# A new order of the seven products of a block, and norm statistics issued two chunks later, in a decoder step of two layers

## Chip, cores and metric

One core of a Trainium2 chip runs the whole step. The metric is device time in microseconds (us), the median of several executions. Engines are named as in the profile: PE (TensorE, matrix products), DVE (VectorE), ACT (ScalarE), POOL (GpSimd), SP (the queue that issues DMAs).

## What is computed

The reference is one inference step of a two-layer decoder for 1024 prompt tokens and 8 samples of 4 tokens, 1056 columns in all, in fp32. Each layer has a recurrent mixer, a cross attention and a feed-forward part with a causal convolution of width 3:

```python
def conv_ffn(h, w_up, conv_w, conv_b, w_down, prev):
    L = h.shape[1]
    up = h @ w_up
    ext = jnp.concatenate([prev.astype(up.dtype), up], axis=1)
    c = conv_b + conv_w[0] * ext[:, 0:L]
    for j in range(1, CONV_W):
        c = c + conv_w[j] * ext[:, j:j + L]
    a, b = jnp.split(c, 2, axis=-1)
    y = (jax.nn.silu(a) * b).astype(h.dtype)
    return y @ w_down, ext[:, L:]
```

`h` is the RMS norm of the 1024-wide residual stream, `w_up` is 1024 x 5632, `w_down` 2816 x 1024. The last two columns of `ext` are the convolution states that are returned.

## The kernel before

**Blocks of seven products.** The feed-forward products go through Strassen's scheme in Winograd's form: a 2x2 block product is made of seven products of sums of blocks. A unit is one pair of 128 output rows. In the up projection (tiles `blu`) there are 21 units a layer, f = 1 to 21, of four 128-row slices of each operand half; in the down projection (`bld`) 20 units a layer, of two slices. The operands are split in a high and a low fp32r part, so each 128x128 piece takes three matmuls (`mm3`, lines 592 to 594). A product has two halves c of 264 columns; one half is a step: 4 x 3 = 12 matmuls in an up unit, 6 in a down unit. A unit has 14 steps, in the order of the list `ORDER` (line 46), run by `products` (line 694).

**Banks.** `PRODUCTS` gives each product its accumulation bank q. Products 1, 6, 7 and 4 add up in bank 0, one after the other, and after each one the sum so far is read out; product 2 has bank 1; products 5 and 3 share bank 2. A product that adds to a bank can't start before the sum that stands there has been read. The reading is `take` in `ffn_take` (up) and `ffn_add` (down): in an up unit ACT copies (line 961), DVE adds (965) and POOL multiplies by the norm factor (966), or DVE does both for product 4 (963). In a down unit DVE adds to the residual (981), or for products 1 and 6 ACT copies (978) and POOL adds (979).

**Weights of the next unit.** `Blocks.steps` is called after each step of a unit and prepares the next one: POOL makes the sums s2, s3 (lines 231, 233), s1 (232) and s4 (237); `parts` splits them, ACT casting the high part (217) and DVE subtracting (218). The tiles `whi/wlo` rotate over two buffers, shared by a11, a12 and by s2, s3; s1, a22 have slots of their own (`wh1/wl1`).

**Convolution of the unit before.** `ffn_conv` queues for each half of the columns an ACT pass (`ct`, line 1002), two DVE multiply-adds a side (1005), the SiLU on ACT (1009), a DVE product (1011) and a store of the row to HBM (`fd`). These are handed out in `tick` as credit of PE time builds up.

**The order on each engine** is not that of the code alone: the framework's scheduler replays the program against its own model and places an instruction where that model finds it ready. Every engine then works through its list strictly in order.

**Norm statistics.** The factor of the feed-forward norm isn't known when the first up projections (`pju`, by `proj`, four chunks of 264 columns each) start. `proj` issues the sums of squares (`stats`, tiles `npsff`) after its first chunk, and `spread` (tiles `dgff`, `nbcff`) after the last chunk of the first projection; the chunks' results wait in their banks until then.

**States.** `conv_state_out` and `conv_last` transpose the convolution states on PE (tiles `cops`) and store them; the last two are issued in the first and the second down unit, in `ffn`.

Of the kernel before, what the change touches and what calls it, by code (L numbers as in the profile page):

```python
# [26 lines left out]
T = TP + TS  # L27
NCH = 3
CH = T // NCH
H = T // 2  # L30
HC = H // 2
# [11 lines left out]


PRODUCTS = {1: ("a11", "b11", 0), 2: ("a12", "b21", 1), 3: ("s4", "b22", 2), 4: ("a22", "t4", 0), 5: ("s1", "t1", 2), 6: ("s2", "t2", 0), 7: ("s3", "t3", 0)}
ORDER = [(1, 0), (1, 1), (2, 0), (6, 0), (6, 1), (2, 1), (7, 0), (7, 1), (5, 0), (5, 1), (4, 0), (4, 1), (3, 0), (3, 1)]
STARTS = (1, 2, 5)
GROUPS = [2,2,2,2,2]
OH = 3
# [1 line left out]
OP = 3  # L51
OB = 3
OG = 2
PREP = {(0, 2): 1, (1, 3): 2, (1, 10): 1, (2, 3): 1, (2, 8): 1, (2, 11): 1, (3, 0): 1, (3, 4): 1, (3, 10): 1, (3, 12): 1}
RL = 2
PA, PB = (2, 6)
# [21 lines left out]
class Task:  # L78


    def __init__(self, gen):
        self.gen, self.done, self.result = gen, False, None
        self.step()
# [119 lines left out]
class Blocks:  # L203
# [19 lines left out]
    def steps(self, at):  # L223
        k, w, n = self.k, self.w, self.name
        gt = k.nc.gpsimd.tensor_tensor
        wt = lambda q: k.wp.tile([P, 1024], F32R, tag=q, name=f"{q}{n}", bufs=2)[:, :2 * w]
        for s in at:
            a, b = self.raw
            if s == 2:
                self.s = k.c(f"ws{n}")[:, :2 * w]  # L230
                gt(out=self.s[:, w:], in0=a[:, :w], in1=b[:, :w], op=ALU.subtract)  # L231
                gt(out=b[:, :w], in0=b[:, :w], in1=b[:, w:], op=ALU.add)  # L232
                gt(out=self.s[:, :w], in0=b[:, :w], in1=a[:, :w], op=ALU.subtract)
            elif s == 6:
                self.parts(a, ("a11", "a12"), wt("whi"), wt("wlo"))
            elif s == 7:
                gt(out=a[:, w:], in0=a[:, w:], in1=self.s[:, :w], op=ALU.subtract)
            elif s == 9:
                t = k.wp.tile([P, 1024], F32R, tag="whi", name=f"whs{n}", bufs=2), k.wp.tile([P, 1024], F32R, tag="wlo", name=f"wls{n}", bufs=2)
                self.parts(self.s, ("s2", "s3"), t[0][:, :2 * w], t[1][:, :2 * w])  # L240
            elif s == 11:
                self.parts(b, ("s1", "a22"), k.c(f"wh1{n}", F32R)[:, :2 * w], k.c(f"wl1{n}", F32R)[:, :2 * w])
            elif s == 12:
                t = k.c(f"w4{n}", F32R)
                self.parts(a[:, w:], ("s4",), t[:, :w], t[:, w:2 * w])
# [39 lines left out]
class Kernel:  # L285
    def __init__(self, tc, ins, outs):
        self.tc, self.nc = tc, tc.nc
        self.i, self.o = ins, outs
        self.fill = []
        self.planned, self.ready = [], {}  # L290
        self.slow, self.credit = [], 0.0
        self.chain, self.owed = None, 0.0
        self.pending = None
        self.vcol = {}
        self.wide, self.odd = False, 0

# [98 lines left out]
    def v(self, nm, j):  # L395
        return self.vcol[nm][:, j:j + 1]
# [199 lines left out]
    def proj(self, w, col, hi, lo, evac, name, width=P, ch=CH):  # L596

        n = len(hi)
        us = 3 * n * ch / 2400.0
        wh, wl = self.wunit(self.wcol(w, col, n, name, width))  # L600
        held = []
        for c in range(T // ch):
            sl = slice(c * ch, (c + 1) * ch)
            ps = self.abank(f"pj{name}{c}")
            for k in range(n):
                self.mm3(ps[:width, :ch], wh[:, k], wl[:, k], hi[k][:, sl], lo[k][:, sl], k == 0, k == n - 1)
            if c == 1:
                self.prefetch()
            if self.pending is None:
                evac(c, ps)  # L610
            else:
                held.append((c, ps))
                if c == 0:
                    self.pending.stats(self.pending.tokens())
                elif c == T // ch - 1:
                    self.pending.spread()
                    self.pending = None
                    for q in held:
                        evac(*q)
            self.tick(us - 0.6)  # L620
            yield us

# [71 lines left out]
    def products(self, weights, acts, n, name, take):  # L694
# [3 lines left out]
        us = 3 * n * HC / 2400.0  # L698
        for s, (p, c) in enumerate(ORDER):
            a, b, q = PRODUCTS[p]  # L700
# [84 lines left out]
    def ffn(self, l, norm, ahead, cuts=None, post=None):  # L785
# [12 lines left out]
        at = 0  # L798
# [55 lines left out]
        for u, (g, m, w) in enumerate(dns):  # L854
            t = self.c(f"dt{w.name}") if SLOWADD else None
            g.run()
            i = groups.index(g) + 1
            for s in self.products(w, g.acts, g.n, w.name, self.ffn_add(m, t)):
                self.ahead(todo, len(ups) + u, s)
                if i < len(groups):  # L860
                    groups[i].run(PREP.get((m // 2, s), 0))
                if u == 0 and s == 6:
                    self.conv_state_out(l, NFT - NFT % 4)
                if u == 1 and s == 6:
                    self.conv_last(l)
                if u == len(dns) - 1 and s == 10:
                    self.tick(1e9)
                    last = self.ffn_rest(l, at)
                yield
# [82 lines left out]
    def ffn_take(self, exts, rstd):  # L952
        nc = self.nc

        def take(p, c, ps):
            q, h = {1: (0, 0), 2: (0, 0), 6: (0, 1), 3: (0, 1), 7: (1, 1), 5: (1, 1), 4: (1, 0)}[p]
            a = h * H + c * HC
            for d, s, v in self.pieces(exts[q], a, HC):
                z, r = v(ps[:, s]), v(rstd[:, a + s.start:a + s.stop])
                if p in (1, 6, 7):  # L960
                    nc.scalar.copy(out=d, in_=z)  # L961
                elif p == 4:
                    nc.vector.tensor_tensor(out=d, in0=z, in1=r, op=ALU.mult)
                else:
                    nc.vector.tensor_tensor(out=d, in0=d, in1=z, op=ALU.add)  # L965
                    nc.gpsimd.tensor_tensor(out=d, in0=d, in1=r, op=ALU.mult)  # L966
            return 0.0 if p in (1, 6, 7) else 0.4
        return take

    def ffn_add(self, m, t):  # L970
# [655 lines left out]
    def heads(self, nm, cur, proj, gates, gname, s0, sp, ss, last, before=None):  # L1626

        self.pt = self.tok(f"pt{nm}")
        self.nc.gpsimd.memset(self.pt, 0.0)
        lz = self.c(f"lz{nm}")  # L1630
        self.nc.gpsimd.memset(lz[:, :1024], 0.0)
        self.ph = lz[:, 512:768].rearrange("p (c i) -> p c i", i=32)
        self.lq = lz[:, :NS * 32].rearrange("p (s c) -> p s c", c=32)
        self.lp = lz[:TS, NS * 32:NS * 32 + 2 * P]
        res = []
        for h in range(4):
            q, k, g, vt, vts = cur
            n = f"{nm}{h}"
            if before is not None:
                before(h)  # L1640
            gt = self.later(gates(h))
            nxt = self.later(proj(h + 1)) if h < 3 else last(res)
            res.append(self.lin(q, k, g, vt, vts, gt, gname, s0[0, :, h], sp[0, 0, h], ss[0, :, h], n))
            if h < 3:
                while not nxt.done:
                    self.gap(1.0)
                cur = nxt.result
        return res
# [8 lines left out]
    def mix_six(self, w, os_, y):  # L1657
        self.plan(self.wrow(w, 4 * P, 2, "mo14"))
        yield 0.0
        yield from self.out_six(w, os_, "mo1", y, OG)  # L1660

# [5 lines left out]
    def gla(self):  # L1667
        rstd = self.next
        hi, lo = rstd.hi, rstd.lo
        self.gla_gate_load()  # L1670
        self.spill()
        w = self.i["w_out_c"][0]

        def last(res):
            os_ = [t for o in res for t in o]
            y = [self.split(t, f"mo1{4 + j}") for j, t in enumerate(os_[4:])]
            self.fill[0].finish()
            self.fill.pop(0)
            self.reload("mx1")
            self.later(self.mix_six(w, os_, y))  # L1680
        proj = lambda h: self.gla_proj(h, hi, lo, rstd)
        gates = lambda h: self.gates(self.i["w_in_c"][0], 2048 + h * 256, 2, hi, lo, rstd, f"gl{h}")
        res = self.heads("gl", self.run(proj(0)), proj, gates, "gla_gnorm", self.i["state_gla"], self.o["gla_p"], self.o["gla_s"], last)
        self.mix_last(w, 6, res[3], 1)
# [570 lines left out]
```

## Time and profile before

| | |
|---|---|
| median of 3 runs | 3276.51 us (3275.88 to 3279.37) |
| the profiled execution | 3273.8 us, its span 3272.0 us |
| PE busy | 3104.0 us, 95% |
| DVE busy | 2427.9 us, 74% |
| ACT / POOL busy | 1460.5 / 1458.8 us |
| mean granted PE clock | 0.984 of full |

The profile shows one execution. Busy shares are means over stages of different kinds, so a stage is read through its own stretch of time. Up units of layer 0 run from 961 to 1412 us, its down units from 1412 to 1656; in layer 1 from 2530 to 2973 and to 3230.

### The profile page before, as it was taken

The page shows a single profiled execution, that of the slowest core. Times are in us where ns is not written, and L with a number is a line of the kernel's source. Part 1 is how long each engine was busy: PE and PEld are TensorE (multiplying, and loading weights), DVE is VectorE, ACT ScalarE, POOL GpSimd, SP SyncE. Part 2 cuts the span into 40 slices and gives each one's busy share as a digit, 9 for nine tenths or more (in the row PEclk, how much of TensorE's full clock was granted, in tenths as well). Part 3 has the DMA queues.
Part 4 walks back from the last instruction along what each step waited for, and adds up shares of the span by engine and source line. Part 5 has one row for each costly group of instructions (what it writes and reads, how often), then busy time and mean ns, then how long its engine had stood idle before and what let it go on. Part 6 is the DMA issues. An engine that isn't in the chain of part 4 may idle for free.

```text
span 3272.0 us, 65208 instructions
## 1 busy us (share of the span) xinstructions
PE 3104.0 (95%) x25741; PEld 2953.6 (90%) x25741; DVE 2427.9 (74%) x4662; ACT 1460.5 (45%) x3008; POOL 1458.8 (45%) x1722
## 2 busy tenths in 40 slices
PE   8999899999989999989999999899999999998998
PEld 7998888998889999988899999889988999998888
DVE  6649977844798887799984444684379977878998
ACT  7122265444464444444443334244446544444445
POOL 4011113200467677778731111340035777678774
PEclk9999999999999999999999999999999999999999
DMA  8513264344222222243231111225332222224322
GB/s 263 186 47 96 84 208 152 112 137 151 78 87 84 79 79 76 71 144 99 79 124 49 50 57 57 79 71 187 101 130 86 87 70 80 77 77 148 99 72 96
DMA packets 367072, 336.07 MB, mean 103 GB/s; under 512 B 30030, under 2 KB 317949, under 8 KB 366765
## 3 DMA queue, kind: packets, MB, share of 16 engines
q1 hardware_dynamic: 366764, 331.90, 31.7%
q8 instruction: 202, 3.31, 0.4%
q14 instruction: 106, 0.86, 0.1%
HBM read 250.60 MB, written 81.24 MB: 101 GB/s over the span
## 4 chain that ended last, share of the span: by engine, by line
PE 49%; DVE 28%; POOL 10%; issue 6%; ACT 5%; DMA 1%; DVEq 0%; SPq 0%; ACTq 0%; POOLq 0%
DVE ct L1005 5%; POOL ext L966 3%; DVE xff L981 2%; PE blu L592 2%; PE pjxq L594 2%; PE pjxq L592 2%; PE pjxq L593 2%; PE blu L594 2%; PE blu L593 2%; ACT ct L1002 2%; DVE ext L965 1%; DVE wlsu L218 1%; POOL wsu L231 1%; POOL wru L232 1%; ACT ct L1009 1%
## 5 line engine op out<-in xcount | busy, mean ns | idle before, releaser
L966 POOL TENSOR_TENSOR ext<-ext,rstdff 128x264 f32<-128x264 f32 (+2 forms) x336 | 299.2, 903 | 207.6 <-DVE ext L965 207.6
L1005 DVE SCALAR_TENSOR_TENSOR ct<-ext,cw,ct 128x528 f32<-128x528 f32 (+1 forms) x352 | 329.0, 956 | 47.2 <-ACT ct L1002 46.4
L979 POOL TENSOR_TENSOR xff<-xff,dtd 128x264 f32<-128x264 f32 x160 | 162.7, 1031 | 74.6 <-ACT dtd L978 74.4
L1002 ACT ACTIVATE ct<-ext,cw 128x544 f32<-128x544 f32 (+1 forms) x176 | 141.3, 830 | 115.6 <-POOL ext L966 83.7
L592 PE MATMUL blu<-hhff,whiu 128*128 128x264 f32 x672 | 192.1, 286 | 0.0
L594 PE MATMUL blu<-hhff,wlou 128*128 128x264 f32 x672 | 191.6, 286 | 0.0
L720 POOL TENSOR_TENSOR o<-o 128x528 f32<-128x528 f32 x4 | 5.4, 1342 | 361.1 <-DVE xo0bb L270 180.5
L981 DVE TENSOR_TENSOR xff<-xff,bld 128x264 f32<-128x264 f32 x400 | 155.5, 418 | 11.3 <-PE bld L594 6.8
L592 PEld LDWEIGHTS blu<-hhff,whiu 128*128 128x128 f32 x672 | 127.9, 190 | 0.0
L594 PEld LDWEIGHTS blu<-hhff,wlou 128*128 128x128 f32 x672 | 127.5, 190 | 0.0
L592 PE MATMUL pjxq<-hhxa,whxq 128*128 128x352 f32 x384 | 126.4, 329 | 0.0
L593 PE MATMUL pjxq<-hlxa,whxq 128*128 128x352 f32 x384 | 125.5, 327 | 0.0
L594 PE MATMUL pjxq<-hhxa,wlxq 128*128 128x352 f32 x384 | 124.9, 325 | 0.0
L965 DVE TENSOR_TENSOR ext<-ext,blu 128x264 f32<-128x264 f32 (+2 forms) x336 | 111.0, 351 | 10.3 <-PE blu L594 5.5
L1009 ACT ACTIVATE ct<-ct 128x528 f32<-128x528 f32 x88 | 57.3, 651 | 136.1 <-DVE ct L1005 136.0
L961 ACT COPY ext<-blu 128x264 f32<-128x264 f32 (+2 forms) x336 | 94.7, 322 | 48.3 <-PE blu L594 48.2
L592 PE MATMUL blu<-hhff,w4u 128*128 128x264 f32 x336 | 96.2, 286 | 4.4 <-DVE ext L965 4.4
L1011 DVE TENSOR_TENSOR ct<-ct 128x528 f32<-128x528 f32 x88 | 88.4, 1005 | 13.1 <-ACT ct L1009 13.1
L593 PE MATMUL blu<-hhff,whiu 128*128 128x264 f32 x336 | 97.0, 289 | 0.0
L593 PE MATMUL blu<-hlff,whiu 128*128 128x264 f32 x336 | 95.6, 284 | 0.0
L594 PE MATMUL blu<-hhff,w4u 128*128 128x264 f32 x336 | 95.5, 284 | 0.0
L593 PE MATMUL blu<-hlff,w4u 128*128 128x264 f32 x336 | 95.5, 284 | 0.0
(2690 smaller groups left out, 13067.0 us busy)
## 6 DMA issues: line engine op xcount, KB each, us to landing
wru<-in_ffn_w_up SPq DMA_DIRECT2D x88, 512.0 KB
wrd<-in_ffn_w_down SPq DMA_DIRECT2D x80, 256.0 KB
wrkv<-in_xa_w_kv SPq DMA_DIRECT2D x32, 512.0 KB
kc<-in_cache_mem_k SPq DMA_DIRECT2D x64, 256.0 KB
vc<-in_cache_mem_v SPq DMA_DIRECT2D x64, 256.0 KB
fd<-ct SPq DMA_DIRECT2D x44, 264.0 KB
fd<-ct SPq DMA_DIRECT2D x44, 248.0 KB
xmx<-xd SPq DMA_DIRECT2D x16, 528.0 KB
```

What stands on the lines that cost most here:

```text
L592: nc.tensor.matmul(ps, wh, ah, start=first, stop=False, **kw)
L593: nc.tensor.matmul(ps, wh, al, start=False, stop=False, **kw)
L594: nc.tensor.matmul(ps, wl, ah, start=False, stop=last, **kw)
L961: nc.scalar.copy(out=d, in_=z)
L965: nc.vector.tensor_tensor(out=d, in0=d, in1=z, op=ALU.add)
L966: nc.gpsimd.tensor_tensor(out=d, in0=d, in1=r, op=ALU.mult)
L979: nc.gpsimd.tensor_tensor(out=x, in0=x, in1=b, op=ALU.add)
L981: nc.vector.tensor_tensor(out=x, in0=x, in1=ps, op=ALU.add)
L1002: nc.scalar.activation(out=ct[q], in_=exts[q][0][:, o:o + w], func=AF.Identity, scale=wv(0, q), bias=wv(3, q))
L1005: nc.vector.scalar_tensor_tensor(out=ct[q], in0=exts[q][0][:, o + j:o + j + w], scalar=wv(j, q), in1=ct[q], op0=ALU.mult, op1=ALU.add)
L1009: nc.scalar.activation(out=a, in_=a, func=AF.Silu)
L1011: nc.vector.tensor_tensor(out=b[:, :n], in0=a[:, :n], in1=b[:, :n], op=ALU.mult)
```

## The change

It reorders the seven products to 1, 2, 6, 5, 7, 3, 4, both halves of one after the other. So a bank's next product stands three steps behind the end of the one before. With product 5 ahead of product 7, its sum is the first that lands in its quarter: in `ffn_take` ACT now copies product 5's and DVE adds product 7's. In `Blocks.steps` the splits of s2, s3 and of s1, a22 change places. In `proj` the statistics come after the third chunk and the spreading after the first chunk of the second projection where chunks are 264 wide (`HC`); for 352 wide chunks (`CH`) nothing changes. The last state transposes go from the first and second down unit to the third and fourth.

```diff
-ORDER = [(1, 0), (1, 1), (2, 0), (6, 0), (6, 1), (2, 1), (7, 0), (7, 1), (5, 0), (5, 1), (4, 0), (4, 1), (3, 0), (3, 1)]
+ORDER = [(p, c) for p in (1, 2, 6, 5, 7, 3, 4) for c in (0, 1)]
...
+STATS, SPREAD = {CH: 0, HC: 2}, {CH: 2, HC: 4}
...
-            elif s == 9:
+            elif s == 11:
                 t = k.wp.tile([P, 1024], F32R, tag="whi", name=f"whs{n}", bufs=2), k.wp.tile([P, 1024], F32R, tag="wlo", name=f"wls{n}", bufs=2)
                 self.parts(self.s, ("s2", "s3"), t[0][:, :2 * w], t[1][:, :2 * w])
-            elif s == 11:
+            elif s == 9:
                 self.parts(b, ("s1", "a22"), k.c(f"wh1{n}", F32R)[:, :2 * w], k.c(f"wl1{n}", F32R)[:, :2 * w])
...
-                held.append((c, ps))
-                if c == 0:
+                self.held.append((evac, c, ps))
+                at = len(self.held) - 1
+                if at == STATS[ch]:
                     self.pending.stats(self.pending.tokens())
-                elif c == T // ch - 1:
+                elif at == SPREAD[ch]:
                     self.pending.spread()
                     self.pending = None
-                    for q in held:
-                        evac(*q)
+                    while self.held:
+                        f, *q = self.held.pop(0)
+                        f(*q)
...
-                if u == 0 and s == 6:
+                if u == 2 and s == 6:
                     self.conv_state_out(l, NFT - NFT % 4)
-                if u == 1 and s == 6:
+                if u == 3 and s == 6:
                     self.conv_last(l)
...
-                if p in (1, 6, 7):
+                if p in (1, 6, 5):
                     nc.scalar.copy(out=d, in_=z)
...
-            return 0.0 if p in (1, 6, 7) else 0.4
+            return 0.0 if p in (1, 6, 5) else 0.4
```

ACT in up unit 6 of layer 0, before. `blu_600` and `blu_601` are the halves of bank 0 of unit 6, `ext_12401` and `ext_12404` its two sides, `wh1u_7` and `whiu_7` weights of unit 7, `ct` the convolution of unit 5. The second pair of copies from bank 0 reads product 6, the third product 7:

```order
L961 COPY ext_12401<-blu_600_12407 128x264
L1002 ACTIVATE ct_12460<-ext_12145,cw_10715 128x544
L961 COPY ext_12401<-blu_601_12426 128x264
L217 CAST wh1u_7_12618<-wru_71_12395 128x1024
L1009 ACTIVATE ct_12460<-ct_12460 128x544
L961 COPY ext_12401<-blu_600_12407 128x264
L961 COPY ext_12401<-blu_601_12426 128x232
L961 COPY ext_12401<-blu_601_12426 128x8x4
L217 CAST whiu_7_12533<-wru_70_12211 128x1024
L961 COPY ext_12404<-blu_600_12407 128x264
```

The same place in the change (`blu_620` is product 5):

```order
L964 COPY ext_12401<-blu_600_12407 128x264
L1012 ACTIVATE ct_12460<-ct_12460 128x544
L219 CAST wh1u_7_12588<-wru_71_12395 128x1024
L964 COPY ext_12401<-blu_601_12426 128x264
L219 CAST whiu_7_12534<-wru_70_12211 128x1024
L964 COPY ext_12401<-blu_600_12407 128x264
L964 COPY ext_12401<-blu_601_12426 128x232
L964 COPY ext_12401<-blu_601_12426 128x8x4
L964 COPY ext_12404<-blu_620_12520 128x264
L219 CAST w4u_7_12639<-wru_70_12211 128x512
```

The cast `wh1u`, which stood ahead of the copies of product 6, now stands ahead of the second copy of product 1, and `whiu` ahead of product 6's.

DVE near the end of up unit 6, before (`blu_620`, `blu_621`: bank 2, first product 5, further down product 3):

```order
L965 TENSOR_TENSOR ext_12404<-ext_12404,blu_620_12556 128x264
L218 TENSOR_TENSOR wlsu_7_12589<-wsu_7_12463,whsu_7_12588 128x1024
L218 TENSOR_TENSOR w4u_7_12636<-wru_70_12211,w4u_7_12636 128x512
L965 TENSOR_TENSOR ext_12404<-ext_12404,blu_621_12571 128x232
L965 TENSOR_TENSOR ext_12404<-ext_12404,blu_621_12571 128x8x4
L1005 SCALAR_TENSOR_TENSOR ct_12681<-ext_12401,cw_10715,ct_12681 128x528
L963 TENSOR_TENSOR ext_12404<-blu_600_12407,rstdff_10894 128x264
L1005 SCALAR_TENSOR_TENSOR ct_12681<-ext_12401,cw_10715,ct_12681 128x528
L963 TENSOR_TENSOR ext_12404<-blu_601_12426,rstdff_10894 128x264
L965 TENSOR_TENSOR ext_12401<-ext_12401,blu_620_12556 128x264
```

The same place in the change (`blu_600`, `blu_601` first product 7, further down product 4):

```order
L220 TENSOR_TENSOR w4u_7_12639<-wru_70_12211,w4u_7_12639 128x512
L968 TENSOR_TENSOR ext_12404<-ext_12404,blu_600_12407 128x264
L968 TENSOR_TENSOR ext_12404<-ext_12404,blu_601_12426 128x232
L968 TENSOR_TENSOR ext_12404<-ext_12404,blu_601_12426 128x8x4
L220 TENSOR_TENSOR wlsu_7_12623<-wsu_7_12463,whsu_7_12622 128x1024
L968 TENSOR_TENSOR ext_12401<-ext_12401,blu_620_12520 128x264
L968 TENSOR_TENSOR ext_12401<-ext_12401,blu_621_12542 128x232
L968 TENSOR_TENSOR ext_12401<-ext_12401,blu_621_12542 128x8x4
L1008 SCALAR_TENSOR_TENSOR ct_12681<-ext_12401,cw_10715,ct_12681 128x528 x2
L966 TENSOR_TENSOR ext_12404<-blu_600_12407,rstdff_10921 128x264
```

Product 3's adds have moved ahead of product 4's, so the unit's last reading is one that POOL takes no part in. `wlsu` stands behind the adds of product 7.

PE at the third group of sums of squares in layer 0, before:

```order
L593 MATMUL pju_03_10869<-hlff_10311,whu_0_10612 128x264
L159 MATMUL npsff_10789<-ones,sqaff_10313 128x2 x3
L594 MATMUL pju_03_10869<-hhff_10303,wlu_0_10613 128x264
L592 MATMUL pju_03_10869<-hhff_10304,whu_0_10612 128x264
L593 MATMUL pju_03_10869<-hlff_10312,whu_0_10612 128x264
```

and in the change:

```order
L595 MATMUL pju_03_10869<-hlff_10311,whu_0_10612 128x264
L161 MATMUL npsff_10845<-ones,sqaff_10313 128x2 x3
L596 MATMUL pju_03_10869<-hhff_10303,wlu_0_10613 128x264
L594 MATMUL pju_03_10869<-hhff_10304,whu_0_10612 128x264
L595 MATMUL pju_03_10869<-hlff_10312,whu_0_10612 128x264
```

The group stands between the same two matmuls in both. Only the second group and the spreading (`nbcff`, 11 and 24 matmuls) have moved back.

## Rows read from the trace of the kernel before

**Rows 1.** The page: span, then busy time of each engine.
```profile
span 3272.0 us, 65208 instructions
...
PE 3104.0 (95%) x25741; PEld 2953.6 (90%) x25741; DVE 2427.9 (74%) x4662; ACT 1460.5 (45%) x3008; POOL 1458.8 (45%) x1722
```

**Rows 2.** Who waited for whom on PE: total us, times, longest us.
```profile
PE bld L592 <- DVE xff L981: 30.7, 32, 1.3
PE blu L592 <- ACT ext L961: 30.5, 25, 1.5
PE npsff L159 <- DVE sqaff L133: 11.5, 2, 5.8
...
PE cops L778 <- POOL cst L991: 6.9, 2, 3.5
```

**Rows 3.** Windows: up units 4 to 20, down units and their starts, layers 0, 1.
```profile
core 0: us, PE busy (x) PEld busy (x) DVE busy (x) ACT busy (x) POOL busy (x), PEclk, DMA share, GB/s
1032.20:1395.90 363.70, 351.41 (x2867) 349.30 (x2866) 291.28 (x437) 169.29 (x309) 260.20 (x341) 1.00 0.24 76
1410.00:1656.00 246.00, 221.09 (x1712) 213.31 (x1712) 229.54 (x383) 108.11 (x235) 187.18 (x185) 0.99 0.32 107
1425.00:1460.00 35.00, 30.62 (x230) 29.58 (x230) 30.78 (x49) 13.78 (x32) 31.20 (x30) 0.95 0.29 98
2597.90:2962.00 364.10, 351.47 (x2867) 349.33 (x2866) 291.06 (x438) 168.08 (x307) 261.17 (x341) 1.00 0.25 76
2973.00:3222.00 249.00, 224.53 (x1730) 217.35 (x1729) 231.96 (x384) 110.15 (x240) 189.56 (x187) 0.98 0.32 106
2990.00:3040.00 50.00, 41.77 (x321) 40.48 (x319) 45.50 (x75) 23.92 (x52) 40.29 (x40) 0.97 0.28 91
```

**Rows 4.** Windows cut at the first matmul of up units 7, 8, 9, 10.
```profile
1097.30:1117.80 20.50, 20.50 (x170) 20.50 (x170) 15.60 (x24) 8.10 (x17) 13.35 (x19) 1.00 0.26 79
1117.80:1140.00 22.20, 20.75 (x171) 20.53 (x170) 18.28 (x29) 11.55 (x21) 17.06 (x21) 1.00 0.25 79
1140.00:1160.40 20.40, 20.40 (x170) 20.40 (x169) 16.05 (x24) 8.20 (x17) 13.22 (x19) 1.00 0.25 80
1160.40:1182.60 22.20, 20.84 (x172) 20.62 (x171) 18.29 (x29) 11.57 (x21) 17.04 (x21) 1.00 0.23 73
sum 85.30, PE 82.48 PEld 82.06 DVE 68.22 ACT 39.42 POOL 60.66; mean PE 20.62 PEld 20.51 DVE 17.06 ACT 9.85 POOL 15.17
```

**Rows 5.** Timeline of unit 8, PE: start us, us, [idle before <-releaser].
```profile
1128.83 0.39 PE L592 MATMUL blu<-ff0t00h,whsu 128*128 128x264 f32 x1 [1.45 <-ACT ext L961]
```

**Rows 6.** The same timeline, ACT.
```profile
1122.12 0.85 ACT L1002 ACTIVATE ct<-ext,cw 128x544 f32<-128x544 f32 x1 [2.07 <-POOL ext L966]
...
1126.91 1.05 ACT L217 CAST wh1u<-wru 128x1024 fp32r<-128x1024 f32 x1 [3.68 <-POOL wru L232]
1127.86 0.65 ACT L1009 ACTIVATE ct<-ct 128x544 f32<-128x544 f32 x1
1128.42 0.71 ACT L961 COPY ext<-blu 128x264 f32<-128x264 f32 x3
```

**Rows 7.** The same timeline, POOL.
```profile
1123.31 1.83 POOL L231 TENSOR_TENSOR wsu<-wru,wru 128x512 f32<-128x512 f32 x1
1125.21 1.66 POOL L232 TENSOR_TENSOR wru<-wru 128x512 f32<-128x512 f32 x1
```

**Rows 8.** Waits of DVE, up units of layer 0: total us, times, longest us.
```profile
DVE ct L1005 <- ACT ct L1002: 21.4, 34, 1.6
...
DVE w4u L218 <- ACT w4u L217: 16.9, 8, 2.1
```

**Rows 9.** Two lines of DVE: duration ns min/median/max, first and last start.
```profile
L1005 DVE SCALAR_TENSOR_TENSOR ct<-ext,cw,ct x352: 751/777/1811, 976.4 to 3213.2; 128x528 f32<-128x528 f32 x126, 128x544 f32<-128x544 f32 x50
...
L965 DVE TENSOR_TENSOR ext<-ext,blu x336: 171/402/433, 975.8 to 2991.4; 128x264 f32<-128x264 f32 x84, 128x32 f32<-128x32 f32 x42, 128x232 f32<-128x232 f32 x42
```

**Rows 10.** Timeline of the start of layer 0's up projection, PE.
```profile
942.16 1.44 PE L159 MATMUL npsff<-ones,sqaff 128*128 128x2 f32 x6 [5.74 <-DVE sqaff L133]
...
952.91 0.49 PE L183 MATMUL nbcff<-dgff,ones 128*128 128x128 f32 x2 [1.17 <-DVE dgff L176]
...
970.54 0.39 PE L594 MATMUL blu<-ff0t00h,wl1u 128*128 128x264 f32 x1 [1.86 <-DVE wl1u L218]
```

More of the change, by code (lines that the diff above doesn't have):

```diff
@@ L292, in __init__ @@
         self.chain, self.owed = None, 0.0
-        self.pending = None
+        self.pending, self.held = None, []
         self.vcol = {}
@@ L600, in proj @@
         wh, wl = self.wunit(self.wcol(w, col, n, name, width))
-        held = []
         for c in range(T // ch):
```

## The prediction

> **What bounds the kernel now.** First the page's engine line: PE is busy 3104.0 us of 3272.0, DVE 2427.9 [rows 1]. So the most that better ordering can give is the 168 us in which PE idles, and only what this change touches of them. Second, the list of PE's waits [rows 2]: the entries that the change can touch are `bld` on DVE (30.7 us), `blu` on ACT's copies (30.5), `npsff` on DVE (11.5) and `cops` on POOL (6.9). The mixers' Strassen products run in the same order, and none of their tiles is in these rows: I put them at nothing.
>
> Third, the stretches. In up units 4 to 20 PE is busy 351.4 of 363.7 us, 21.39 a unit, with the clock at 1.00 [rows 3]. Cut at each unit's first matmul, the units alternate: 20.50, 22.20, 20.40, 22.20 us [rows 4]. The short ones are PE's floor, 168 matmuls without a gap, 0.122 us each, 1.46 us a step. The long ones idle at one place: 1.45 us ahead of product 7, for ACT's copy of product 6 [rows 5]. Why is that copy late? ACT's list says it: the copies stand behind the cast `wh1u`, which waited 3.68 us for POOL's sum `wru` [rows 6], and that sum ended at 1125.21 + 1.66 = 1126.87, 9.07 us after the unit's start at 1117.80, behind `wsu` of 1.83 us [rows 7]. So the up stage is not short of any engine; one engine's list is in an unlucky order in every second unit.
>
> The down stage is another case: DVE is busy 229.5 of 246.0 us and 232.0 of 249.0, PE only 221.1 and 224.5 [rows 3]. DVE is the bound there, and only its own idle time, 16.5 + 17.0 = 33.5 us, can be had.
>
> **The change, up units.** The old order alternates because the scheduler placed conv work of the unit before differently in even and odd units; the new one has all units alike. Product 7 now comes behind product 5: 36 matmuls (4.4 us) lie between product 6's end and product 7's start, where there were 29 (3.5 us) in the long units, counted in PE's list. The sum `wru` itself comes earlier: POOL reaches it after the unit before has its readings behind it, and product 3's adds come two steps, 2.9 us, sooner. From 9.07 that makes 6.15 us after the unit's start. Now the new list on ACT: `wh1u` stands ahead of the second copy of product 1, which releases the second half of product 6, 61 matmuls or 7.45 us into the unit. The cast takes 1.05 us [rows 6], one half's copy 0.36, half of the 0.71 for three pieces of which the first is one half [rows 6]; so `wru` may end until about 6.0 us. 6.15 against 6.0: this is close, a stall of 0.15 us a unit at worst in this reckoning, and none if odd units' earlier start holds.
>
> With PE free, who is next? DVE. Its busy time in a unit is 15.60 to 18.29, mean 17.06 us [rows 4]. To that come waits its list holds by itself: for ACT's `ct` pass 21.4 us over 17 units, 1.26 a unit, and for ACT's part of `w4u` 16.9 over 8, 2.1 each [rows 8]. 17.06 + 1.26 + 2.1 = 20.4. If the two halves' `ct` passes of 0.85 us each [rows 6] are both waited for in full, 1.7 takes the place of 1.26: 20.9. I take 20.7 between the two, just above PE's floor. So a unit goes from 21.39 to 20.7, −0.69; over 36 units (the 34 of both windows and one more a layer from those at the ends) −25 us. Bounds: PE's floor of 20.5 gives −0.89 x 36 = −32; no gain gives 0; the losses are among the rivals.
>
> The swap of the two `parts` calls moves the ACT casts and DVE subtractions `wlsu`, 1024 wide, behind product 7's adds; it issues the same instructions. The copies of product 5 on ACT and the adds of product 7 on DVE are the old ones of 7 and 5 with names exchanged: nothing. No DMA is added; POOL's and SP's lists keep their entries.
>
> **Down units.** The same order there; a unit's readings by DVE don't get fewer. What goes is what idles DVE. The last `cops` transposes make PE wait 3.5 us twice [rows 2]; around them DVE idles 35.0 − 30.78 = 4.2 and 50.0 − 45.5 = 4.5 us [rows 3], because it has no product to read. Two units later, POOL's `cst` will be long done: −8.7. Of the other 25 us of DVE's idle time I count 1.3, since product 3 no longer follows on the bank of product 5 with only two steps between: −10 together. Bounds: 0, and −20 if half of the rest goes as well. That the clock is granted at 0.95 and 0.97 around the transposes [rows 3] would add about a microsecond; it stays inside these bounds.
>
> **Head of the feed-forward.** The third group of sums of squares stands between the same two matmuls as before, so its wait of 5.74 us for `sqaff` [rows 10] stays, twice. The second group and the spreading move 11 and 24 matmuls back; the spreading's wait of 1.17 us would go, but the first `blu` matmul waits 1.86 us for `wl1u` at 970.54 behind it [rows 10], and what is saved ahead is waited there. So 0, with −11.5 (both waits gone) as the other end.
>
> **Sum.** 3273.8 (the profiled execution) − 25 − 10 = 3238.8. The median of the runs, 3276.5, lies 2.7 above that execution: 3241.
>
> **Rivals.**
>
> *DVE's round becomes the bound, and the kernel is slower.* The long units carry 18.28 us of DVE work, the short ones 15.60 [rows 4], since multiply-adds (L1005) move from one to the other and their price changes: 751 ns at the least, 777 in the middle, 1811 at the most, while the adds of L965, which have one input from a bank, never pass 433 [rows 9]. If the even order puts every unit at 18.28, the round is 18.28 + 1.7 + 2.1 = 22.1, +0.7 a unit: +25 − 10, 3291 us. It decides from a DVE round of 21.4. For it: product 5's `wlsu` and the multiply-adds now stand together while POOL makes the weight sums. Against it: the mean of two units carries the same instructions, and readings moved ahead leave `ct` nothing new to wait for. The Trainium skill ("SBUF — State Buffer", Who interferes with whom) has the mechanism: a DVE instruction with two SBUF inputs contends with a GpSimd instruction that reads SBUF. The trace agrees in kind (1811 against 433 ns [rows 9]); by that rule alone the round would lie nearer 22.1 than 20.7, as more of those multiply-adds would meet POOL's sums.
>
> *ACT's head is blocked in every unit.* If `wru` still ends 9.07 us into the unit, the cast ends at 10.1, and product 6's second half, wanted at 7.45, starts at 10.5: 3.0 us lost in each, 23.5 a unit, +76 − 10, 3342 us. It decides from `wru` ending at 6.9 us, where the loss equals today's mean stall of 0.89. Against it: product 3's adds come 2.9 us sooner.
>
> *PE's floor.* DVE follows without trouble in the short units (15.60 and 16.05 of 20.4); if so in all, −32, and the down stage gives 15 to 20: about 3224.
>
> *Only the down stage gains.* ACT's wait is replaced by another of the same length, at product 5 or 3: 3273.8 − 10 + 2.7 = 3266.
>
> *The statistics don't do what is said.* The later issue moves the group of 5.74 us past no matmul; this is in the forecast already, at nothing.
>
> **How the numbers follow.** Forecast with its own range (3228 to 3256): 0.55. PE's floor: 0.15. Only the down stage: 0.13. DVE's round: 0.12. ACT's head: 0.05. The range 3212 to 3272 takes the first three and what the bounds of the head can add below (3224 − 11.5); the two slower cases, 0.17, are left out. A measurement of this kernel tells 0.2%, 6.5 us, from no change: below 3270 is faster, above 3283 slower. From the third case 0.03 goes to no change, and 0.02 from the edge of the fourth: faster 0.80, same 0.05, slower 0.15.
>
> **What would show it.** Right: up units all alike at 20.5 to 20.9 us in the windows, `blu` on ACT's `ext` under 5 us in the list of PE's waits, `cops` on `cst` gone, `npsff` still at 11.5, down stages of about 241 and 244 us, DVE busy around 17 us in each up unit. Wrong: alternating units, a new entry of `blu` waiting for DVE's `ext` over 20 us (first rival), `wru` ending later than 6.9 us after a unit's start with PE idle ahead of product 6's second half (second), or a median outside 3212 to 3272.

## The result and the profile after

| | before | after |
|---|---|---|
| median of 4 runs each | 3276.2 us (3272.98 to 3279.37) | 3242.48 us (3238.84 to 3243.13) |
| ratio, 95% interval | | 0.9895 [0.9878, 0.9912] |
| the profiled execution, its span | 3273.8, 3272.0 us | 3238.8, 3237.1 us |

The two profiled executions lie 35.0 us apart, the medians 33.7. First the page of the change, with the lines that answer to [rows 1]:

```profile
span 3237.1 us, 65350 instructions
...
PE 3101.1 (96%) x25741; PEld 2952.3 (91%) x25741; DVE 2446.9 (76%) x4662; ACT 1454.7 (45%) x3008; POOL 1468.3 (45%) x1722
```

PE does the same work; DVE is busy 19 us longer with the same 4662 instructions. Next the list of PE's waits, as in [rows 2] (total us, times, longest us):

```profile
PE bld L596 <- DVE wlod L220: 15.0, 13, 2.0
PE npsff L161 <- DVE sqaff L135: 12.0, 2, 6.3
PE bld L594 <- DVE xff L984: 10.6, 10, 1.7
PE bld L594 <- ACT whid L219: 7.9, 3, 3.9
...
PE blu L596 <- DVE wl1u L220: 6.5, 2, 3.3
```

The waits of `blu` for ACT's `ext` (30.5 us before) are 2.0 us now, below the rows shown. `cops` is gone; a wait of 3.9 us of `bld` for ACT's `whid` is new. `npsff` stays. Where the time went is read from windows that begin at the same instructions in both traces. In the kernel before, up units 1 to 3 and then unit 21 with the down units, layer 0 and layer 1 (columns as in [rows 3]):

```profile
961.16:1032.17 71.01, 65.06 (x508) 63.48 (x506) 68.51 (x90) 36.95 (x65) 53.34 (x63) 0.98 0.26 79
1395.91:1662.20 266.29, 241.28 (x1869) 233.13 (x1868) 247.71 (x412) 119.24 (x257) 198.41 (x196) 0.99 0.34 112
2529.49:2600.48 70.99, 65.95 (x508) 64.52 (x507) 68.47 (x90) 37.03 (x65) 53.35 (x63) 0.95 0.25 78
2964.64:3230.40 265.76, 241.29 (x1863) 234.11 (x1862) 247.14 (x409) 117.99 (x254) 197.47 (x196) 0.98 0.32 107
```

In the change, with the stretch of up units 4 to 20 of layer 0 and layer 1, which answers to [rows 3], as the second and fifth line:

```profile
954.81:1028.16 73.35, 66.28 (x508) 65.01 (x507) 69.24 (x96) 37.97 (x67) 51.86 (x68) 0.95 0.27 80
...
1028.16:1379.56 351.40, 351.07 (x2867) 349.65 (x2866) 299.62 (x436) 166.06 (x306) 268.03 (x343) 1.00 0.26 78
...
1379.56:1639.50 259.94, 240.34 (x1864) 234.38 (x1862) 246.28 (x410) 118.49 (x255) 197.18 (x195) 0.97 0.34 114
2512.78:2586.24 73.46, 65.55 (x507) 64.28 (x506) 69.52 (x96) 38.01 (x68) 51.88 (x68) 0.95 0.26 80
...
2586.24:2937.53 351.29, 350.98 (x2867) 349.74 (x2866) 300.77 (x436) 166.04 (x306) 269.27 (x343) 1.00 0.26 78
...
2937.53:3195.00 257.47, 239.97 (x1863) 233.91 (x1862) 245.34 (x409) 118.70 (x255) 197.74 (x195) 0.98 0.33 111
```

Up units 4 to 20 gave 12.3 and 12.9 us, unit 21 with the down units 6.3 and 8.3; units 1 to 3 cost 2.3 and 2.5. That is −35.0 for the two feed-forward parts, as much as the whole difference. Outside them the two executions differ too, but it cancels: the first up unit begins 6.4 us earlier in the change (954.81 for 961.16), and the stretch between the two parts is 6.0 us longer (1639.50 to 2512.78 for 1662.20 to 2529.49). That is scatter as far as these runs tell: with the order of the change alone (the first experiment) the first up unit began at 961.85.

In these steady units PE is now busy 351.07 of 351.40 us. It is at its floor, and the floor is 351.07 / 17 = 20.65 us a unit, not the 20.5 of the best single units: the transposes that stand among them have their share. DVE's waits in the same stretch are these two, the whole list:

```profile
DVE w4u L220 <- ACT w4u L219: 30.3, 17, 1.9
DVE ct L1008 <- ACT ct L1005: 21.0, 35, 2.0
```

Before, the list had among others the wait behind POOL's late sum:

```profile
DVE wl1u L218 <- ACT wh1u L217: 20.3, 9, 2.3
```

In the change, busy 299.62 + 30.3 + 21.0 = 350.9 of 351.4 us: DVE waits for nobody but ACT, three times a unit, and its round, the time that its own list takes for a unit, is 20.64 us. PE's floor and DVE's round have met; whether DVE has any slack left, the list can't say, and an experiment below does. POOL in unit 7 of the change, which begins at 1090.90, to be held against [rows 7]:

```profile
1092.17 1.29 POOL L233 TENSOR_TENSOR wsu<-wru,wru 128x512 f32<-128x512 f32 x1
1093.54 1.66 POOL L234 TENSOR_TENSOR wru<-wru 128x512 f32<-128x512 f32 x1
```

`wru` ends 4.30 us into the unit; before, it ended at 9.07 in the long unit 8 and at 7.5 in the short unit 7. In the change it ends at 4.0 to 5.2 in all seventeen units.

### The profile page after: what moved, and what is told of

Its sections match the earlier page's. It is cut to its first block, busy times and chain, and to the rows that moved or that the text cites. A ratio compares the mean times of both kernels' runs of the same rounds, so it can differ in the third digit from the quotient of the medians.

```text
span 3237.1 us, 65350 instructions
## 1 busy us (share of the span) xinstructions
PE 3101.1 (96%) x25741; PEld 2952.3 (91%) x25741; DVE 2446.9 (76%) x4662; ACT 1454.7 (45%) x3008; POOL 1468.3 (45%) x1722
## 5 line engine op out<-in xcount | busy, mean ns | idle before, releaser
L969 POOL TENSOR_TENSOR ext<-ext,rstdff 128x264 f32<-128x264 f32 (+2 forms) x336 | 358.7, 1093 | 122.2 <-DVE ext L968 121.9
L1008 DVE SCALAR_TENSOR_TENSOR ct<-ext,cw,ct 128x528 f32<-128x528 f32 (+1 forms) x352 | 370.5, 1089 | 47.4 <-ACT ct L1005 45.6
L968 DVE TENSOR_TENSOR ext<-ext,blu 128x264 f32<-128x264 f32 (+2 forms) x336 | 104.4, 350 | 0.0
L219 ACT CAST w4u<-wru 128x512 fp32r<-128x512 f32 x42 | 26.1, 621 | 149.9 <-POOL wru L239 141.6
L1400 POOL TENSOR_TENSOR khg<-khg,tothg 128x512 f32<-128x512 f32 (+1 forms) x24 | 31.8, 1325 | 123.1 <-PE shg L1371 53.1
```

What stands on the lines that cost most here:

```text
L219: nc.scalar.copy(out=hi, in_=src)
L1008: nc.vector.scalar_tensor_tensor(out=ct[q], in0=exts[q][0][:, o + j:o + j + w], scalar=wv(j, q), in1=ct[q], op0=ALU.mult, op1=ALU.add)
L1400: nc.gpsimd.tensor_tensor(out=kv, in0=kv, in1=tv[:, :, 1:2].to_broadcast([P, nb, m]), op=ALU.mult)
```

## Experiments

**The order alone.**

```diff
-STATS, SPREAD = {CH: 0, HC: 2}, {CH: 2, HC: 4}
+STATS, SPREAD = {CH: 0, HC: 0}, {CH: 2, HC: 3}
...
-                if u == 2 and s == 6:
+                if u == 0 and s == 6:
...
-                if u == 3 and s == 6:
+                if u == 1 and s == 6:
```

> The change without its two later parts: only the order of products, with the reading of 5 and 7 and the two splits; statistics and last states stand as in the kernel before. Theory (the order gives nearly all, and the later states uncover another wait at the same place): 3240 to 3246 us, the cops wait of 3.5 us twice is there and the first down units lose no more than in the change. Rival (the later states are worth 8 us, as the prediction had it): 3249 to 3252. If the loss of 2.4 us a layer in up units 1 to 3 of the change comes from the later spreading, those three units take 71.0 here as before; if it comes from the order, 73.4.

3242.21 us, ratio 0.9894 [0.9876, 0.9912]: all of the gain, as the change. The `cops` wait that was expected didn't come: with the transposes at their old place PE waited for the weights `whid` instead, up to 3.9 us, as in the change.

```profile
PE bld L594 <- ACT whid L219: 8.4, 3, 3.9
```

The first three units took 71.7 and 72.2 us (1033.59 − 961.85 and 2594.28 − 2522.12; the profiled execution was the slowest of the four, 3249.43 us). So of the 2.3 and 2.5 us that the change loses there a third to a half comes from the order, and the rest with the later spreading.

**The later states alone,** in the kernel before.

```diff
-                if u == 0 and s == 6:
+                if u == 2 and s == 6:
...
-                if u == 1 and s == 6:
+                if u == 3 and s == 6:
```

> The kernel before with only the last state transposes in the third and fourth down unit. Theory: the cops wait goes, and PE waits at the first down unit for operand sums of DVE instead; 3274 to 3277 us, no difference. Rival (the prediction's term): 3267 to 3269, 8.7 us less.

3274.42 us, 0.9992 [0.9984, 1.0001]: at most some 5 us, and no difference that can be told. The prediction's 8.7 us aren't there. Why, this run shows in its first down unit, where PE had waited 3.45 us ahead of the transposes. PE, then ACT:

```profile
1420.34 0.39 PE L592 MATMUL bld<-y00b,whid 128*128 128x264 f32 x1 [1.19 <-ACT whid L217]
1422.42 0.40 PE L594 MATMUL bld<-y00b,wlod 128*128 128x264 f32 x1 [1.33 <-DVE wlod L218]
```

```profile
1419.14 0.63 ACT L517 CAST y00t11h<-y00r 128x528 fp32r<-128x528 f32 x1 [5.71 <-DVE y00r L723]
1419.67 0.61 ACT L217 CAST whid<-wrd 128x512 fp32r<-128x512 f32 x1
```

2.5 of the 3.45 us are waited for weights now, and PE's waits for ACT's `dtd` in the down units of layer 0 rose from 1.8 to 5.8 us. In the change the same place looks like this, PE and ACT:

```profile
1408.04 0.59 PE L594 MATMUL bld<-y00b,whid 128*128 128x264 f32 x1 [3.88 <-ACT whid L219]
```

```profile
1406.83 0.63 ACT L519 CAST y00t11h<-y00r 128x528 fp32r<-128x528 f32 x1 [4.53 <-DVE y00r L726]
1407.37 0.61 ACT L219 CAST whid<-wrd 128x512 fp32r<-128x512 f32 x1
```

PE stops in its first down unit for 3.88 us, where it stopped for 3.45 before. In both runs the weights `whid` stand on ACT behind a cast that waits for DVE's operand sums (`y00r`). The transposes were only the last of several late results.

**The later statistics alone,** in the kernel before.

```diff
+STATS, SPREAD = {CH: 0, HC: 2}, {CH: 2, HC: 4}
...
-                if c == 0:
+                at = len(self.held) - 1
+                if at == STATS[ch]:
...
-                elif c == T // ch - 1:
+                elif at == SPREAD[ch]:
```

> The kernel before with only the later norm statistics and spreading. Theory: the third group waits its 5.74 us as before, the spreading's wait goes, and the first up unit waits for wl1u that much longer; within 2 us of before, 3275 to 3278. Rival: 3264 to 3270, one or both waits of 5.74 us gone. If the later spreading costs the first three up units 2.4 us a layer, 3280.

3277.19 us, 0.9998 [0.9988, 1.0007]: nothing. `npsff` waits 11.5 us as before, and `blu` for `wl1u` 6.6 us instead of 3.7: what the spreading no longer waits, the first unit does. Units 1 to 3 of layer 0 take 1.6 us longer (72.64 us), which is the rest of what the change loses there.

**The two splits back at their old steps,** in the change.

```diff
-            elif s == 11:
+            elif s == 9:
                 t = k.wp.tile([P, 1024], F32R, tag="whi", name=f"whs{n}", bufs=2), k.wp.tile([P, 1024], F32R, tag="wlo", name=f"wls{n}", bufs=2)
...
-            elif s == 9:
+            elif s == 11:
                 self.parts(b, ("s1", "a22"), k.c(f"wh1{n}", F32R)[:, :2 * w], k.c(f"wl1{n}", F32R)[:, :2 * w])
```

> The change with the two splits at their old steps (s2, s3 at 9, s1, a22 at 11). ACT's list in the up units is the same as in the change, only DVE's wlsu stands elsewhere. Theory: nothing depends on it, 3239 to 3246 us. Rival (the splits' order keeps DVE's round short): up units over 20.9 us, 3250 or more.

3255.2 us, 0.9937 [0.9921, 0.9953]. Neither expectation holds: the time is the rival's, but the place isn't. Up units 4 to 20 and then unit 21 with the down units of layer 0:

```profile
1033.56:1384.96 351.40, 351.06 (x2867) 349.67 (x2866) 299.60 (x436) 166.05 (x306) 268.16 (x343) 1.00 0.26 78
1384.96:1648.70 263.74, 239.33 (x1863) 231.31 (x1862) 243.77 (x410) 118.52 (x255) 197.63 (x195) 0.99 0.34 112
```

The up units are the same to 0.01 us; the down stage is 3.8 us longer (259.94 in the change), 3.8 in layer 1 too. The medians differ by 12.7 us. Of the 13.2 us between the two profiled executions 7.6 lie in the down stages and 5.4 ahead of the first up unit, which began at 954.81 us in the change and at 960.22 here; but that start lies between 954.8 and 961.9 us over all the runs, so whether those 5.4 us belong to the swap stays open. Then the swap alone, in the kernel before:

```diff
-            elif s == 9:
+            elif s == 11:
...
-            elif s == 11:
+            elif s == 9:
```

> The kernel before with only the two splits changed over (s1, a22 at step 9, s2, s3 at 11). If the swap is worth by itself what the change lost without it, some 13 us, mostly in the down units: 3262 to 3268. If its worth hangs on the new order: within 4 us of before, 3273 to 3281.

3271.99 us, 0.9987 [0.9975, 0.9998], between the two cases: some 4 us by itself. Unit 21 with the down units took 265.57 and 265.46 us, 0.7 and 0.3 less than before. So in the down units the swap is worth 7.6 us with the new order and 1.0 without.

**The cast out of ACT's way,** in the kernel before: `wh1`'s split moves from step 11 to 13, the last.

```diff
-            elif s == 11:
+            elif s == 13:
                 self.parts(b, ("s1", "a22"), k.c(f"wh1{n}", F32R)[:, :2 * w], k.c(f"wl1{n}", F32R)[:, :2 * w])
```

> The kernel before, its order of products untouched, with the split of s1 and a22 four steps... after the unit's last step instead of step 11. On ACT the cast wh1u then stands behind the copies of product 6, not ahead. Theory (the stall ahead of product 7 is ACT's list, not the distance between products of one bank): the 1.45 us in every second unit goes, units 4 to 20 of a layer take 351 to 355 us instead of 363.7, the whole 3249 to 3258. Rival (product 7 comes too soon behind product 6 on the same bank, whatever ACT's list): a stall of over 1 us ahead of product 7 stays in at least every second unit, 3270 to 3290.

3291.04 us, 1.0044 [1.0032, 1.0057], slower, and neither expectation holds. The alternation ended, but not the stall: ahead of product 7 every unit now waits, 0.4 to 0.9 us, where every second one had waited 1.0 to 1.5. In units 4 to 20 that is 10.3 us where it had been 12.3:

```profile
PE blu L592 <- ACT ext L961: 10.3, 17, 0.9
```

Product 7 and, ahead of it, ACT in unit 7:

```profile
1110.83 0.39 PE L592 MATMUL blu<-ff0t00h,whsu 128*128 128x264 f32 x1 [0.87 <-ACT ext L961]
```

```profile
1107.07 0.84 ACT L1002 ACTIVATE ct<-ext,cw 128x544 f32<-128x544 f32 x1 [4.16 <-POOL ext L966]
1107.81 0.36 ACT L961 COPY ext<-blu 128x264 f32<-128x264 f32 x1
1109.79 0.66 ACT L1009 ACTIVATE ct<-ct 128x544 f32<-128x544 f32 x1 [1.62 <-DVE ct L1005]
```

The cast is gone from ahead of the copies; a convolution pass and a SiLU stand there instead and wait for POOL and DVE. Units 4 to 20 take 363.54 us, as before (363.70). The 15 us lost in all lie in units 1 to 3 (74.99 for 71.01 in layer 0) and in the down stages (270.79 for 266.29 in layer 0). So the cast stood in the way in the kernel before, but taking it away only let others stand there.

**Products 7 and 5 the other way round,** then **4 ahead of 3,** in the change.

```diff
-ORDER = [(p, c) for p in (1, 2, 6, 5, 7, 3, 4) for c in (0, 1)]
+ORDER = [(p, c) for p in (1, 2, 6, 7, 5, 3, 4) for c in (0, 1)]
...
-                if p in (1, 6, 5):
+                if p in (1, 6, 7):
```

> The change with products 7 and 5 the other way round: 1, 2, 6, 7, 5, 3, 4, with the reading of before (ACT copies product 7's, DVE adds product 5's). Product 3 is still ahead of 4 and POOL's sums early, but 7 stands right behind 6 on bank 0 and 3 right behind 5 on bank 2. Theory A (the distance between products of a bank is what counts): a stall ahead of product 7 or 3 of 0.3 to 1.0 us in a unit, up units 20.9 to 21.7, the whole 3250 to 3280 us. Theory B (the early sums, through product 3 ahead of 4, do it alone): up units as in the change, 20.7, and 3240 to 3247.

3276.0 us, 1.0 [0.9988, 1.0012]: the whole gain is gone. The time is theory A's; its stalls are there only in part, for in units 4 to 20 PE waits 6.9 us for readings of banks, and they are 10.1 us longer than in the change. Then the last two products:

```diff
-ORDER = [(p, c) for p in (1, 2, 6, 5, 7, 3, 4) for c in (0, 1)]
+ORDER = [(p, c) for p in (1, 2, 6, 5, 7, 4, 3) for c in (0, 1)]
```

> The change with its last two products the other way round: 1, 2, 6, 5, 7, 4, 3. Product 5 is still ahead of 7, three steps lie between 6 and 7 and between 5 and 3; 4 stands right behind 7 on bank 0, and product 3's adds and POOL's multiplies come last again. Theory (what makes wru early is product 3 ahead of 4): wru ends at 7 us or later, not 4.3, up units of 21.0 to 22.2, the whole 3250 to 3295. Rival (5 ahead of 7 is what counts): up units of 20.7, 3240 to 3247.

3265.63 us, 0.9965 [0.9952, 0.9977]. The time is the theory's, its reason isn't: `wru` ends 6.06 us into unit 7, not at 7 or later. So product 3 ahead of product 4 accounts for some 1.8 us of the earlier `wru`, and with it behind, `wru` is still earlier than in the kernel before. Units 4 to 20 of both runs, the first with 7 ahead of 5, the second with 4 ahead of 3:

```profile
1035.64:1397.13 361.49, 354.49 (x2867) 350.41 (x2866) 323.54 (x435) 169.12 (x306) 246.98 (x340) 1.00 0.24 75
```

```profile
1030.19:1392.46 362.27, 353.25 (x2867) 350.23 (x2866) 337.21 (x435) 165.66 (x306) 257.18 (x340) 1.00 0.24 75
```

With as many instructions as in the change, DVE is busy 323.5 and 337.2 us, not 299.6. The next three runs ask what DVE's time is worth and what lengthens its instructions.

**DVE's `wlsu` twice; POOL's `wsu` three times; two POOL memsets ahead of it,** each in the up units of the change.

```diff
-        nc.vector.tensor_tensor(out=lo, in0=src, in1=hi, op=ALU.subtract)
+        for _ in range(2 if self.name[0] == 'u' and names == ('s2', 's3') else 1):
+            nc.vector.tensor_tensor(out=lo, in0=src, in1=hi, op=ALU.subtract)
```

> The change with DVE's wlsu made twice in each up unit, 1.1 to 1.4 us more of DVE work. The prediction's reckoning (DVE's own round is 20.7 us and bounds the unit): units of 21.7 to 22.1, 40 to 60 us more, 3280 to 3300. Rival (PE's floor bounds the unit, which is 20.67 us with the transposes among it, and DVE has slack): units of 20.7 to 21.0, 3240 to 3255.

```diff
-                gt(out=self.s[:, w:], in0=a[:, :w], in1=b[:, :w], op=ALU.subtract)
+                for _ in range(3 if self.name[0] == 'u' else 1):
+                    gt(out=self.s[:, w:], in0=a[:, :w], in1=b[:, :w], op=ALU.subtract)
```

> The change with POOL's sum wsu made three times in each up unit, so that wru ends some 3 us later, at 7.0 to 7.5 us after a unit's start, as in the short units of before. DVE's list is not lengthened, POOL's by 3 us of 20.7. ACT then has wh1u and whiu ahead of the copies of product 6. Theory (the three steps to product 7 are slack that takes this up): wh1u ends at 8.5, the copies at 10, product 7 is due at 11.7; units of 20.6 to 21.0, 3240 to 3255 us. Rival (a late wru stalls PE wherever product 7 stands): over 21.5 a unit, 3270 or more.

```diff
+                for _ in range(2 if self.name[0] == 'u' else 0):
+                    k.nc.gpsimd.memset(self.s, 0.0)
                 gt(out=self.s[:, w:], in0=a[:, :w], in1=b[:, :w], op=ALU.subtract)
```

> The change with two POOL memsets of wsu (128x1024) ahead of the sum in each up unit, in place of the two repeated sums: POOL is kept from wru for some 2 to 4 us again, but reads nothing meanwhile, and ACT's list in an up unit is that of the run with repeated sums. Theory (the repeated sums cost 2.2 us a unit because DVE's instructions grew longer beside POOL's reads, its multiply-adds from 1.10 to 1.25 us and wl1u from 1.21 to 1.97): here DVE's busy time stays at 17.6 us a unit and the units under 21.0, 3240 to 3255 us. Rival (POOL's late sums stop ACT, and ACT stops PE): units near 22.9 again, 3320 to 3345.

3289.16 us (1.0042 [1.0026, 1.0059]), 3340.38 (1.0196 [1.018, 1.0213]) and 3299.39 (1.0071 [1.0049, 1.0093]), in the order of the heading. The first is as the prediction's reckoning has it. In the second the rival's time came, but not for the rival's reason; in the third neither time came. Units 4 to 20 of layer 0, one run each, in this order:

```profile
1032.37:1403.28 370.91, 359.22 (x2868) 351.50 (x2866) 319.37 (x455) 165.91 (x306) 284.99 (x345) 1.00 0.25 74
```

```profile
1041.88:1429.32 387.44, 361.67 (x2868) 357.82 (x2866) 337.59 (x432) 165.14 (x306) 296.80 (x371) 0.98 0.23 70
```

```profile
1033.46:1408.64 375.18, 354.73 (x2867) 350.47 (x2866) 318.72 (x435) 165.99 (x306) 278.28 (x375) 1.00 0.23 73
```

Length less DVE's busy time is 51.5, 49.9 and 56.5 us; in the change it is 51.8. DVE's list of waits holds the same two entries in each of the four and none for PE; in the second run:

```profile
DVE w4u L220 <- ACT w4u L219: 34.0, 17, 2.1
DVE ct L1009 <- ACT ct L1006: 15.1, 31, 2.0
```

So the unit's length is DVE's work plus 2.9 to 3.3 us in which it waits for ACT. The first run is the test of slack: 19.75 us more of DVE work (1.16 a unit) made the stretch 19.5 us longer, so DVE had none left. And the second run issues not one more DVE instruction than the change: its 38 us more of DVE's busy time are instructions that grew longer. (PE's mean granted clock is 0.98 of full there; PE is busy 10.6 us longer, but DVE waits for it nowhere.)

What makes them longer, the run with the memsets shows in one unit. DVE's six multiply-adds, then POOL:

```profile
1101.53 0.79 DVE L1010 SCALAR_TENSOR_TENSOR ct<-ext,cw,ct 128x544 f32<-128x544 f32 x1 [0.68 <-ACT ct L1007]
1102.57 0.78 DVE L1010 SCALAR_TENSOR_TENSOR ct<-ext,cw,ct 128x544 f32<-128x544 f32 x1
1103.56 1.51 DVE L1010 SCALAR_TENSOR_TENSOR ct<-ext,cw,ct 128x528 f32<-128x528 f32 x1 [0.21 <-ACT ct L1007]
1104.99 1.82 DVE L1010 SCALAR_TENSOR_TENSOR ct<-ext,cw,ct 128x544 f32<-128x544 f32 x1
1106.73 1.81 DVE L1010 SCALAR_TENSOR_TENSOR ct<-ext,cw,ct 128x528 f32<-128x528 f32 x1
1108.46 0.77 DVE L1010 SCALAR_TENSOR_TENSOR ct<-ext,cw,ct 128x544 f32<-128x544 f32 x1
```

```profile
1100.82 1.96 POOL L234 MEMSET wsu<- 128x1024 f32 x2
1102.86 1.64 POOL L235 TENSOR_TENSOR wsu<-wru,wru 128x512 f32<-128x512 f32 x1
1104.58 1.64 POOL L236 TENSOR_TENSOR wru<-wru 128x512 f32<-128x512 f32 x1
1106.30 1.67 POOL L237 TENSOR_TENSOR wsu<-wru,wru 128x512 f32<-128x512 f32 x1
```

The first, beside a memset, takes 0.79 us, hardly more than the median of 0.777 in [rows 9]. The three that begin while POOL makes a sum take 1.51, 1.82 and 1.81 us; the last, which begins after the last sum has ended at 1107.97, takes 0.77. The second began before the first sum (1102.86) and ran on beside it, and it kept its 0.78 us. All through up units 4 to 20 of that run it is the same: the 51 multiply-adds that began while POOL was at none of its instructions with two inputs took 0.77 to 0.79 us, the 17 that ran on into a sum among them; the 86 that began while it was at one took up to 1.82. The memsets themselves cost DVE nothing; they pushed the sums into later multiply-adds, three of them here.

The rule that the prediction drew on says that a DVE instruction with two SBUF inputs contends with a GpSimd instruction that reads SBUF, "not with one that only writes it" (the Trainium skill, "SBUF — State Buffer", Who interferes with whom). The trace agrees with both halves: 1.51 to 1.82 us beside the sums, 0.79 beside the memset.

So part of the theory held (memsets don't slow DVE), and its forecast of the time didn't, since it took the sums to stay where they were.

**Half of product 5 from DVE to ACT and POOL in the down units** (and in the mixers' products), a try at a faster kernel.

```diff
-                if p in SLOWADD:
+                if p in SLOWADD or (p, c) == (5, 0):
...
-            return 0.0 if p in SLOWADD else 0.4
+            return 0.0 if p in SLOWADD or (p, c) == (5, 0) else 0.4
```

> The change with the first half of product 5 in the down units (and in the mixers' products) read by ACT and added by POOL, as products 1 and 6 are, not by DVE. It takes some 20 DVE adds of 0.42 us, 8 us, from each down stage, and gives POOL 20 adds of 1.0 us on top of 181 of 240 us. Theory (DVE bounds the down stage): 4 to 8 us a layer less, 3226 to 3236. Rival (what DVE gains goes to longer two-input instructions beside POOL's additional reads, or to waits for POOL's adds): within 6 us of the change, 3237 to 3249, or slower.

3267.29 us, 0.9971 [0.9961, 0.998]: 25 us behind the change. Its down units of layer 0 (the change has 239.50 us with DVE busy 227.78 there):

```profile
1405.30:1653.70 248.40, 220.37 (x1694) 212.22 (x1694) 227.70 (x367) 114.90 (x253) 202.10 (x200) 0.99 0.30 99
```

Some 20 DVE adds fewer, and DVE is busy as long as in the change; it waits 9.1 us for PE there, for 3.0 in the change. What was taken from DVE came back as longer instructions. That POOL's 20 more adds made them so fits the run with the memsets, but was not tested by itself here. The rival was right, and no run was clearly faster than the change.

## Why the prediction was right, point by point

**Sum.** Forecast −35 against the profiled execution, measured −35.0; forecast a median of 3241, measured 3242.5. The up units were forecast by the right mechanism. That the sum came out so closely is luck: the up units gave 20.4 us in all instead of 25, the down units with unit 21 gave 14.6 instead of 10, and about half of what the down units gave came from a term put at nothing (the swap of the splits), while the main one that was counted gave nothing that can be told.

**Up units, −25.** Units 4 to 20 gave 0.73 and 0.76 us a unit, forecast 0.69. Two steps held: the copy of product 6 no longer stands behind a late `wru` (4.30 us into the unit, forecast 6.15), and DVE's round is what comes next, 20.64 us by its busy time and waits, forecast 20.7. Adding DVE work showed it: 1.16 us in, 1.15 us longer. The parts of the round are not those of the forecast: 17.6 us busy, 1.2 for `ct` and 1.8 for `w4u`, where 17.06, up to 1.7 and 2.1 were added up; too little work and too much waiting made up for each other. What was wrong is the floor of PE: 20.65, not 20.5, as the 351.4 us of PE's busy time in [rows 3] already said. So for the up units "PE's floor" was no case of its own; it is the forecast. And the step "36 units (the 34 of both windows and one more a layer from those at the ends)" failed: units 1 to 3 lost 2.3 and 2.5 us.

**Why the order helps** was told too simply. "One engine's list is in an unlucky order" is true of the kernel before, but another list on ACT in the old order left the unit at 21.4 us, and both other orders of the products left it at 21.3. Whether the distance between products of a bank or the place of POOL's sums among DVE's instructions counts for more, these runs don't separate: each order moved both.

**Down units, −10.** The total was −14.6 with unit 21, and the term that made up most of the forecast failed: "Two units later, POOL's `cst` will be long done: −8.7." It was done, and PE stopped in the first down unit for `whid`. The later states are worth nothing that can be told: alone they gave no clear difference, and the change without them and without the later statistics has the same time. "Of the other 25 us of DVE's idle time I count 1.3" was far too little: the waits of `bld` for `xff` went from 30.7 to 10.6 us, while those for `wlod` rose from 4.4 to 15.0. By the windows of unit 21 and the down units, DVE's idle time fell from 18.6 us in either layer to 13.7 and 12.1.

**The swap of the splits, "it issues the same instructions": nothing.** Wrong: without it the change is 12.7 us slower, and 7.6 of the 14.6 us of the down units are its part.

**Head, 0.** Right: `npsff` still waits 12.0 us (11.5 before), and the first unit waits longer for `wl1u` (3.3 us, 1.9 before).

**The rivals.** The first, DVE's round at 22.1, named the right resource. The multiply-adds did get longer, from a median of 777 to 985 ns, and DVE's work in a unit rose from 17.1 to 17.6 us; it needed a round of 21.4, and the round stopped at 20.64. The sums made three times and the memsets took it past that point (387.44 / 17 = 22.8, 375.18 / 17 = 22.1). The second, ACT's list blocked in every unit at 3342 us, did not come: `wru` ends early. (The 3340 us of the sums made three times are near it, but by DVE's longer instructions.) "Only the down stage gains", where one wait for ACT takes the place of another, did not come either: PE waits 0.3 us for ACT in units 4 to 20 of layer 0. It is what the late split showed in the old order.

## What to carry to other kernels

When a stall goes, add up the next engine's busy time and the waits it doesn't share with the stalled one; that sum is an estimate of the new length, and it can be checked by giving the engine a microsecond more. Before counting a removed wait as gained, look at what else is late at that place: here the weights behind it were nearly as late. Two steps that change places issue the same instructions and can still be worth as much as the term that was reckoned. And an engine's instruction times aren't constants of the instruction: moving work to POOL, or moving it in time, moves DVE's durations.

## What was not expected of the hardware

Two more sums of POOL in a unit (28.8 us more of POOL's busy time over 17 units, 1.7 a unit) lengthened DVE's work by 2.2 us a unit and the unit by 2.1, with no DVE instruction added. The effect depends on who runs beside whom and on who began first: the same multiply-add took 0.79 us beside a memset, 0.78 when it began ahead of a sum, and 1.51 to 1.82 when it began while POOL made one.
